# A decoder layer in split precision: first weights loaded and split ahead of constants and squares, the last tile's gate in column groups, spilled activations loaded two blocks earlier

## The chip, the cores and the metric

The kernel runs on one core of one Trainium2 chip. The core has a matrix engine (TensorE, PE in the rows; its weight loads, which overlap matmuls, are listed as PEld), a vector engine (VectorE, DVE), a scalar engine (ScalarE, ACT), GpSimd (POOL) and a sync engine (SyncE, SP), which here issues every plain DMA. Each engine works through its own instructions in program order and waits on semaphores. The metric is device time in microseconds of one execution.

## The reference

One decoder layer for 512 prompt tokens and 64 sample tokens (8 sequences of 8), width 1024, in fp32:

```python
xn = rms_norm(x, attn_norm_g)
z = xn @ w_in                                    # q, k, v, su, sv, gate_a, gate_b
a = window_attention(q, k, v); m = gelu(su) * sgu(layer_norm(gelu(sv)))
h = sigmoid(g_a) * (a @ w_branch_a) + sigmoid(g_b) * (m @ w_branch_b)
x1 = x + h @ w_out
x2 = x1 + peer(rms_norm(x1))                     # see below
gate = sigmoid(rms_norm(x2) @ w_ple_gate)
x3 = x2 + gate * (p_i @ w_ple)
```

`peer` is a product-key retrieval over 16,384 single-neuron experts: 8 heads, the best 16 of each; a token's result is the sum over its experts of gate times gelu(u . x) times the row v.

## The kernel before

**Split matrices.** Every large product is made of three matmuls on fp32r parts: high times high, high times low, low times high. `load_block` (L69) is one weight block of 128 x 1024: a DMA by SP into a ring of four buffers `w_raw`, then `split` (L65): ACT writes `w_hi` (L66, a rounded copy), DVE subtracts to get `w_lo` (L67). These two have a priority offset of 1000 in the scheduler, which sets the order of each engine's instructions when the program is built. Weight blocks pass in the order in which they are written, 3 buffers of `w_hi` and `w_lo` each.

**Start.** x comes transposed as 8 chunks of 128 x 576 (`xT`, names c in the rows; 576 = 512 + 64 tokens). ACT squares them (L140), DVE adds the squares (L142); ACT scales each chunk by the norm's weights and rounds it (L181), DVE makes the low part (L182). PE sums the squares over partitions (L151, each waits for all eight), and a few small steps (L153 to L187) make `rn`, the factor by which each column of a product is multiplied when it leaves PSUM (L192). `w_chunk` (c = 0 to 29) is the projection by one block of 128 columns of `w_in`: 24 matmuls of 256 columns into one PSUM bank, then 24 of 320 into another (`joint`, `tform`, L82), k innermost. `mm` has two banks, so chunk 1 overwrites what chunk 0 had in them. Chunk 0 is k, chunk 1 is v, chunks 2 to 5 are q; after chunk 2 PE transposes v (L249).

**Middle.** Attention, the gating unit, the merge, the expert query and the top-k follow; a long part of it is bound by DVE. Then the prompt's last three tiles of 128 tokens go through all experts densely, 128 blocks of 128 experts: `stage1` makes the activations of a block (`peer_uT`, `xd` in the rows), and `stage2` (the loop over j) multiplies them with the gates `gs` (L974), splits them into `wh` (ACT) and `wl` (DVE) and multiplies by a block of `peer_v` into six PSUM banks `oacc` (L939, 18 matmuls of 512 columns). The other tile and the sample tokens are done by gathers on POOL (`row`, L707) and multiply-adds on DVE (L719), woven in.

**Spilled activations.** The activations of 19 blocks (j = 2, 4, ..., 38) don't fit in SBUF and are in DRAM (`ad`). At the top of the loop over j, the block j + 2 is loaded back (L946, names `x1c<-ad`) into a pool whose x1c tile has 3 buffers. A buffer is read last by the low split `wl<-x1c` of its block. Every 8 blocks SP loads `gs`, 1.5 MB.

**End.** For five tiles (sample, gathered prompt tile, three dense tiles) `tail_gate` (L902) multiplies the normed x2 by `w_pg`, k outermost, both 512-column halves; `tail_out` then does per half a sigmoid (L909), a multiply (L910), an add (L911) and a store (L912).

Of the kernel before, what the change touches and what calls it, by code (L numbers as in the profile page):

```python
# [7 lines left out]
F32 = mybir.dt.float32  # L8
# [3 lines left out]
AF = mybir.ActivationFunctionType  # L12
ALU = mybir.AluOpType
# [15 lines left out]
SPILL = set(range(2, 40, 2))  # L29
# [12 lines left out]
HALVES = (slice(0, 256), slice(256, 576))  # L42
# [5 lines left out]
def tile_decoder_step(ctx: ExitStack, tc: tile.TileContext, a, o):  # L48
    nc = tc.nc
    V, A, T, G, S = nc.vector, nc.scalar, nc.tensor, nc.gpsimd, nc.sync  # L50
# [9 lines left out]
    def cload(name, shape, pl=None):  # L60
        t = (pl or const).tile(shape, F32, name="c_" + name, bufs=1)
        S.dma_start(t, a[name])
        return t
# [2 lines left out]
        A.activation(hi, src, AF.Copy)  # L66
        V.tensor_sub(lo, src, hi.bitcast(F32))  # L67

    def load_block(src, shape=(P, KC, P)):  # L69
        raw = wp.tile(list(shape), F32, name="w_raw", bufs=4)  # L70
        S.dma_start(raw, src)
        hi = wp.tile(list(shape), F32R, name="w_hi", bufs=3)
        lo = wp.tile(list(shape), F32R, name="w_lo", bufs=3)
        with tc.high_priority(offset=1000):
            split(raw, hi, lo)
        return hi, lo

# [14 lines left out]
    def mm():  # L92
        return psM.tile([P, 512], F32, name="mm")
# [7 lines left out]
    pld = dr.tile([NT, D], F32, name="pld")  # L101
    ad = dr.tile([NSP, P, NB], F32, name="ad")
# [16 lines left out]
    def f8(mk, *args):  # L119
        t = [mk(*args), mk(*args)]  # L120
        return [t[k // 4][:, k % 4, :] for k in range(KC)]
# [4 lines left out]
    def bank(tag):  # L126
        return psB.tile([P, 512], F32, name=tag)

    def joint(w, x, out, wk=0, nk=KC, bk=mm):
        for cols in HALVES:  # L130
            ps = bk()[:, :cols.stop - cols.start]
            tform(ps, w, [[xi[k][:, cols] for k in range(nk)] for xi in x], wk, nk)
            out(ps, cols)
# [34 lines left out]

    vecs = cload("vecs", [P, 18])
    xT = f8(f4)  # L170
    for k in range(KC):
        S.dma_start(xT[k], a["xT"][k])
        if k == 1:
            first = load_block(a["w_in"][0])
    ident = cload("ident", [P, P])
    xn = (f8(x4), f8(x4))
    tot, add = sumsq()
    for k in range(KC):
        with tc.high_priority(offset=500):
            add(k, xT[k])  # L180
        A.activation(xn[0][k], xT[k], AF.Copy, scale=vecs[:, k:k + 1])  # L181
        V.scalar_tensor_tensor(xn[1][k], xT[k], vecs[:, k:k + 1], xn[0][k].bitcast(F32),  # L182
                               op0=ALU.mult, op1=ALU.subtract)
    rn = e1.tile([P, NT], F32, name="rn", bufs=1)
    with tc.high_priority(offset=500):
        for cols, ps in rstd_rows(tot, lambda: bank("sc")):
# [2 lines left out]
    def w_chunk(c, dst, out):  # L189
        def scaled(ps, cols):  # L190
            with tc.high_priority(offset=1000):
                V.tensor_tensor(dst[:, cols], ps, rn[:, cols], op=ALU.mult)  # L192
            out(cols)
        joint(load_block(a["w_in"][c]) if c else first, xn, scaled)

    kraw, vTr = tt(), tt()
    w_chunk(0, kraw, lambda cols: None)
# [40 lines left out]
    for g in range(4):  # L238
# [7 lines left out]
        if g == 0:  # L246
            pv = bank("pt")
# [3 lines left out]
            pv = bank("pt")  # L251
# [206 lines left out]
    for i in range(24):  # L458
        if i < 8:
            t, g = (svT, suT)[i // 4], i % 4  # L460
            z = t[:, g, :]
            w_chunk(6 + i, z, lambda cols: A.activation(z[:, cols], z[:, cols], AF.Gelu_apprx_tanh))
        else:
            c, br = divmod(i - 8, 2)
            if (i - 8) % 4 == 0:
                sg4.append(f4())
            sg = sg4[-1][:, (i - 8) % 4, :]
# [15 lines left out]
    hs = ([], [])  # L483
    for c in range(KC):
        w = load_block(a["w_br"][c])
        for i, (x, k0_) in enumerate(((ahl, 0), (mhl, 4))):
            sg = sgs[2 * c + i]
# [20 lines left out]
    for c in range(KC):  # L508
        w = load_block(a["w_out"][c])
# [18 lines left out]
    for c0, r in tilesA:  # L528
# [4 lines left out]
        for hh in range(2):  # L533
            hs = slice(hh * 512, (hh + 1) * 512)
            pt = bank("pt")
            for k in range(4):
                x1k = x1[hh * 4 + k][:, c0:c0 + r]
                T.transpose(out=pt[:r, k * P:(k + 1) * P], in_=x1k, identity=ident)
                if r == NS:
# [3 lines left out]
                                   op0=ALU.mult, op1=ALU.mult)  # L543
# [186 lines left out]
    for i in range(16):  # L730
        h, c = i // 4 + i % 2 * 4, i // 2 % 2
        w = load_block(a["peer_wq"][2 * h + c])
# [134 lines left out]
    d3 = pool(ds, "d3", 3)  # L867
# [27 lines left out]
    def tail_scale(x2, ss, r, xn3):  # L895
        V.scalar_tensor_tensor(xn3[:r], x2[:r], ss[:r], pg[:r], op0=ALU.mult, op1=ALU.mult)

    def tail_gate(w, xh, xl, r, ps):
        for k in range(KC):
            for xi, wi in ((xh, 0), (xh, 1), (xl, 0)):  # L900
                for hh in range(2):
                    T.matmul(ps[hh][:r], lhsT=xi[:, k, :r], rhs=w[k][wi][:, hh * 512:(hh + 1) * 512],  # L902
                             start=k == 0 and xi is xh and wi == 0, stop=k == KC - 1 and xi is xl)

    def tail_out(x2, r, c0, ps, sg, pl):
        S.dma_start(pl[:r], pld[c0:c0 + r])
        for hh in range(2):
            hs = slice(hh * 512, (hh + 1) * 512)
            A.activation(sg[:r, hs], ps[hh][:r], AF.Sigmoid)  # L909
            V.tensor_tensor(sg[:r, hs], sg[:r, hs], pl[:r, hs], op=ALU.mult)  # L910
            V.tensor_tensor(sg[:r, hs], sg[:r, hs], x2[:r, hs], op=ALU.add)  # L911
            S.dma_start(o["y"][c0:c0 + r, hs], sg[:r, hs])  # L912
# [28 lines left out]

    tails, spp, back = [], [], {}
    for j in range(NJ):
        if j + 2 in SPILL:
            back[j + 2] = d3.tile([P, NB], F32, name="x1c")
            S.dma_start(back[j + 2], ad[sorted(SPILL).index(j + 2)])  # L946
        if j and j - 1 not in SPILL and j1 < NJ:
            stage1()
        pay(G2[0] if j1 < NJ else G2[1])
        if j == TAIL0:  # L950
            aLs.close()
            xds.close()
            spp.append(pool(sps, "spare", 2, "right"))
            gather(max(0, P - done[0]), mark_pe[0])
            pg = gp.tile([P, D], F32, name="xr")
            S.dma_start(pg, a["ple_g"])
            tails.append(gathered(0))
        if j == TAIL1:
            gather(1000, mark_pe[0])
        if j == NJ - 2:  # L960
            tails.append(gathered(1))
        if j % JB == 0:
            gsl = gsp[(j // JB + 1) % 2].tile([P, NB // TB, JB, TB], F32, name="gs")
            nb = NB // TB if j else NB // TB - 1
# [12 lines left out]
        split(wf, wh, wl)
        held.append((j, wh, wl, *vw))
        if j != NJ - 2:
            for t in range(3):  # L980
                for hj in held:
                    stage2(t, *hj)
            held.clear()
        if max(SPILL) < j <= max(SPILL) + KC:
            add_x1(j - max(SPILL) - 1)
# [3 lines left out]
    ws = []  # L989
# [21 lines left out]
    banks = [[mm(), mm()]] + [[psC.tile([P, 512], F32, name="oacc") for _ in range(2)] for _ in range(4)]  # L1011

    def finish_tile(i, x2, xh, xl, sg, r, c0):
        tail_gate(ws, xh, xl, r, banks[i])
        tail_out(x2, r, c0, banks[i], sg, tw.tile([P, D], F32, name="pl"))

    finish_tile(0, *tails[1])
    for t, (x2, xn3, ss) in enumerate(xs):
# [110 lines left out]
```

## Time and profile before

| | us |
|---|---|
| median of 3 runs | 1782.16 |
| the three runs | 1780.88, 1782.16, 1788.48 |
| profiled execution | 1776.88 |
| its span in the trace | 1775.1 |

The rows below come from the profiled execution: its span is 1.78 us shorter than its own time, and the median is 5.28 us above that time. Times in rows are us from the start of the span.

### The profile page before, as it was taken

Reading aid. Unit: us, or ns where it says so; the run is one execution under the profiler, and the core shown is the slowest. Engines: PE = TensorE matmul, PEld = TensorE weight load, DVE = VectorE, ACT = ScalarE, POOL = GpSimd, SP = SyncE. Lnnn points to the kernel's source line nnn. Section 1 sums busy time; section 2 is a strip of 40 time slices with the busy share of each in tenths; the row PEclk is TensorE's granted clock in tenths of the full one; section 3 lists DMA queues with packets and bytes.
Section 4 is the critical chain, followed back from the end, with each engine's and each line's share of the span. In section 5 each row is a group of like instructions: output and inputs, shape, how many; then the busy total and the mean of one; then the engine's idle time right before and its main releaser. Section 6 shows DMA issues by size and latency. Waiting matters only on the chain.

```text
span 1775.1 us, 27763 instructions
## 1 busy us (share of the span) xinstructions
PE 1744.3 (98%) x10094; PEld 1575.1 (89%) x10094; DVE 1434.0 (81%) x2876; ACT 867.0 (49%) x1525; POOL 525.9 (30%) x390
## 2 busy tenths in 40 slices
PE   7999999999999899999999999999999999999998
PEld 7988999999999899999988887899899899887876
DVE  6455556548999999999898888998888888999862
ACT  6567444343236698999833333333333333333441
POOL 0000000000002112455245554454544554566300
PEclk9999999999999999999999999999999999999999
DMA  7211233443226577999999999999999999999741
GB/s 242 75 60 38 71 105 122 141 152 106 81 92 225 173 244 235 361 350 355 352 388 367 371 388 364 394 410 369 365 338 360 364 334 331 335 379 376 284 132 70
DMA packets 176457, 457.06 MB, mean 257 GB/s; under 512 B 15552, under 2 KB 76736, under 8 KB 174272
## 3 DMA queue, kind: packets, MB, share of 16 engines
q1 hardware_dynamic: 120736, 253.22, 40.6%
q0 software_dynamic: 55584, 202.07, 30.8%
q8 instruction: 79, 1.29, 0.3%
q14 instruction: 58, 0.48, 0.1%
HBM read 420.18 MB, written 35.78 MB: 257 GB/s over the span
## 4 chain that ended last, share of the span: by engine, by line
PE 77%; issue 7%; DVE 6%; DMA 5%; POOL 3%; ACT 1%; SPq 0%; DVEq 0%; POOLq 0%; ACTq 0%
PE mm L82 36%; PE oacc L939 21%; PE pv L82 5%; POOL row L707 3%; PE sc L822 2%; DMA row<-peer_v,idx 2%; PE pt L822 2%; PE oacc L902 2%; DVE w_lo L67 2%; PE sc L82 1%; DMA x1c<-ad 1%; DVE row L719 1%; DMA row<-peer_u,idx 1%; PE sc L580 1%; PE pv L447 1%
## 5 line engine op out<-in xcount | busy, mean ns | idle before, releaser
L66 ACT ACTIVATE w_hi<-w_raw 128x1024 fp32r<-128x1024 f32 x325 | 343.9, 1059 | 372.9 <-PE mm L82 287.1
L707 POOL DMA_INDIRECT row<-peer_u,idx x192 | 261.1, 1360 | 872.0 <-issue 520.8
L67 DVE TENSOR_TENSOR w_lo<-w_raw,w_hi 128x1024 fp32r<-128x1024 f32 x325 | 396.6, 1221 | 74.0 <-ACT w_hi L66 73.7
L82 PE MATMUL mm<-xd,w_hi 128*128 128x384 f32 x1552 | 405.9, 341 | 0.5 <-ACT w_hi L66 0.5
L82 PE MATMUL mm<-x,w_hi 128*128 128x256 f32 (+1 forms) x1600 | 329.7, 300 | 9.8 <-ACT x L181 9.5
L707 POOL DMA_INDIRECT row<-peer_v,idx x192 | 263.3, 1372 | 231.8 <-DVE acc L726 202.8
L82 PEld LDWEIGHTS mm<-xd,w_hi 128*128 128x128 f32 x1552 | 281.6, 189 | 5.9 <-ACT w_hi L66 0.8
L82 PEld LDWEIGHTS mm<-x,w_hi 128*128 128x128 f32 x1600 | 257.8, 190 | 24.1 <-ACT x L181 10.0
L82 PE MATMUL mm<-xd,w_lo 128*128 128x384 f32 x776 | 264.4, 341 | 3.7 <-DVE w_lo L67 3.7
L726 DVE SCALAR_TENSOR_TENSOR acc<-row,wts,acc 128x1024 f32<-128x1024 f32 x192 | 245.8, 1280 | 5.3 <-DMA row<-peer_v,idx 4.9
L939 PE MATMUL oacc<-w_hi,wl 128*128 128x512 f32 x768 | 242.0, 397 | 3.7 <-DVE wl L67 3.6
L939 PE MATMUL oacc<-w_lo,wh 128*128 128x512 f32 x768 | 242.0, 396 | 0.4 <-DVE w_lo L67 0.4
L939 PE MATMUL oacc<-w_hi,wh 128*128 128x512 f32 x768 | 242.3, 396 | 0.0
L719 DVE SCALAR_TENSOR_TENSOR row<-row,xr 128x1024 f32<-128x1024 f32 x192 | 231.6, 1221 | 11.0 <-DMA row<-peer_u,idx 8.6
L82 PE MATMUL mm<-x,w_lo 128*128 128x256 f32 (+1 forms) x800 | 236.6, 296 | 0.0
L939 PEld LDWEIGHTS oacc<-w_hi,wl 128*128 128x128 f32 x768 | 144.3, 188 | 39.6 <-DVE wl L67 5.5
L939 PEld LDWEIGHTS oacc<-w_lo,wh 128*128 128x128 f32 x768 | 144.4, 188 | 35.5 <-DVE w_lo L67 1.7
L939 PEld LDWEIGHTS oacc<-w_hi,wh 128*128 128x128 f32 x768 | 143.7, 188 | 29.4 <-ACT xr L921 0.8
L82 PEld LDWEIGHTS mm<-x,w_lo 128*128 128x128 f32 x800 | 151.7, 190 | 1.1 <-issue 0.8
L82 PEld LDWEIGHTS mm<-xd,w_lo 128*128 128x128 f32 x776 | 147.0, 189 | 4.7 <-DVE w_lo L67 4.7
L82 PE MATMUL pv<-xd,w_hi 128*128 128x384 f32 x496 | 136.7, 348 | 0.7 <-ACT x L776 0.7
L66 ACT ACTIVATE wh<-x 128x384 fp32r<-128x384 f32 x66 | 34.7, 526 | 162.6 <-PE oacc L939 153.1
(304 smaller groups left out, 2308.8 us busy)
## 6 DMA issues: line engine op xcount, KB each, us to landing
w_raw<-peer_uT SPq DMA_DIRECT2D x128, 512.0 KB
w_raw<-peer_v SPq DMA_DIRECT2D x128, 512.0 KB
gd<-gs SPq DMA_DIRECT2D x24, 1024.0 KB
gs<-gd SPq DMA_DIRECT2D x15, 1536.0 KB
w_raw<-w_in SPq DMA_DIRECT2D x30, 512.0 KB
w_raw<-peer_wq SPq DMA_DIRECT2D x16, 512.0 KB
w_raw<-w_br SPq DMA_DIRECT2D x8, 512.0 KB
w_raw<-w_out SPq DMA_DIRECT2D x8, 512.0 KB
```

Of the source, the lines that this page charges most:

```text
L66: A.activation(hi, src, AF.Copy)
L67: V.tensor_sub(lo, src, hi.bitcast(F32))
L82: mark_pe[0] = T.matmul(ps, lhsT=w[wi][:, wk + k, :], rhs=x[xi][k], start=i == 0, stop=i == n - 1)
L447: T.matmul(ps[:r], lhsT=xi[:, k, :r], rhs=wl_[k][wi][:, hh * 512:(hh + 1) * 512], start=i == 0, stop=i == 5)
L580: T.matmul(ps[:, b * P:(b + 1) * P], lhsT=qp[:, b * P:(b + 1) * P], rhs=sk, start=True, stop=True)
L707: ins = G.indirect_dma_start(out=row_, out_offset=None, in_=table, in_offset=bass.IndirectOffsetOnAxis(ap=ix, axis=0))
L719: V.scalar_tensor_tensor(row_, row_, 1.0, xrs[ti], op0=ALU.mult, op1=ALU.mult, accum_out=dots[:, s:s + 1])
L726: V.scalar_tensor_tensor(accs[ti], row_, wts[:, s:s + 1], accs[ti], op0=ALU.mult, op1=ALU.add)
L822: T.matmul(pt[:, t * P:(t + 1) * P], lhsT=oa[:, t, :], rhs=ob[:, t, :], start=True, stop=True)
L902: T.matmul(ps[hh][:r], lhsT=xi[:, k, :r], rhs=w[k][wi][:, hh * 512:(hh + 1) * 512], start=k == 0 and xi is xh and wi == 0, stop=k == KC - ...
L939: mark_pe[0] = T.matmul(oacc[t][hh], lhsT=wi[:, ts], rhs=vi[:, hh * 512:(hh + 1) * 512], start=j == 0 and last == 0 and vi is vh, stop=j = ...
```

## The change

Three parts. At the start, the block 0 of `w_in` is loaded ahead of x and blocks 1 and 2 ahead of most constants; the scaling and rounding of x gets priority 1500, the squares keep 500; block 0's product runs with k outermost over both halves (new line L205), so that it uses each chunk of x as it comes; chunks 1 and 2 use the PSUM banks `pv` and `pt`, so that they needn't wait until chunk 0 has been scaled. In stage 2, spilled block j + 4 is loaded at the top of the loop instead of j + 2 (at j = 0, blocks 2 and 4). At the end, the last tile's gate is made in three groups of 512, 256 and 256 columns, each with its own 24 matmuls, and the load of `pl` is issued ahead of them.

```diff
-    def load_block(src, shape=(P, KC, P)):
+    def load_block(src, shape=(P, KC, P), urgent=True):
...
-        with tc.high_priority(offset=1000):
+        with tc.high_priority(offset=1000 if urgent else 0):
             split(raw, hi, lo)
...
+    first = [load_block(a["w_in"][0])]
     for k in range(KC):
         S.dma_start(xT[k], a["xT"][k])
-        if k == 1:
-            first = load_block(a["w_in"][0])
+    first.append(load_block(a["w_in"][1]))
     ident = cload("ident", [P, P])
+    first.append(load_block(a["w_in"][2], urgent=False))
...
     for k in range(KC):
-        with tc.high_priority(offset=500):
+        with tc.high_priority(offset=1500):
+            A.activation(xn[0][k], xT[k], AF.Copy, scale=vecs[:, k:k + 1])
+            V.scalar_tensor_tensor(xn[1][k], xT[k], vecs[:, k:k + 1], xn[0][k].bitcast(F32),
+                                   op0=ALU.mult, op1=ALU.subtract)
+    with tc.high_priority(offset=500):
+        for k in range(KC):
             add(k, xT[k])
-        A.activation(xn[0][k], xT[k], AF.Copy, scale=vecs[:, k:k + 1])
-        V.scalar_tensor_tensor(xn[1][k], xT[k], vecs[:, k:k + 1], xn[0][k].bitcast(F32),
-                               op0=ALU.mult, op1=ALU.subtract)
...
-        joint(load_block(a["w_in"][c]) if c else first, xn, scaled)
+        w = first[c] if c < 3 else load_block(a["w_in"][c])
+        if c:
+            joint(w, xn, scaled, bk=(mm, lambda: bank("pv"), lambda: bank("pt"))[c] if c < 3 else mm)
+            return
+        pss = [mm()[:, :cols.stop - cols.start] for cols in HALVES]
+        for k in range(KC):
+            for ps, cols in zip(pss, HALVES):
+                for i, (wi, xi) in enumerate(((0, 0), (0, 1), (1, 0))):
+                    T.matmul(ps, lhsT=w[wi][:, k, :], rhs=xn[xi][k][:, cols], start=k == 0 and i == 0,
+                             stop=k == KC - 1 and i == 2)
+        for ps, cols in zip(pss, HALVES):
+            scaled(ps, cols)
...
-    def tail_out(x2, r, c0, ps, sg, pl):
-        S.dma_start(pl[:r], pld[c0:c0 + r])
-        for hh in range(2):
-            hs = slice(hh * 512, (hh + 1) * 512)
-            A.activation(sg[:r, hs], ps[hh][:r], AF.Sigmoid)
+    def tail_out(x2, r, c0, sg, pl, parts):
+        for p, hs in parts:
+            A.activation(sg[:r, hs], p[:r, :hs.stop - hs.start], AF.Sigmoid)
...
     for j in range(NJ):
-        if j + 2 in SPILL:
-            back[j + 2] = d3.tile([P, NB], F32, name="x1c")
-            S.dma_start(back[j + 2], ad[sorted(SPILL).index(j + 2)])
+        for jb in (2, 4) if j == 0 else (j + 4,):
+            if jb in SPILL:
+                back[jb] = d3.tile([P, NB], F32, name="x1c")
+                S.dma_start(back[jb], ad[sorted(SPILL).index(jb)])
...
-        tail_gate(ws, xh, xl, r, banks[i])
-        tail_out(x2, r, c0, banks[i], sg, tw.tile([P, D], F32, name="pl"))
+        pl = tw.tile([P, D], F32, name="pl")
+        S.dma_start(pl[:r], pld[c0:c0 + r])
+        parts = list(zip(banks[i], (slice(0, 512), slice(512, D))))
+        groups = [parts]
+        if i == 4:
+            groups = [parts[:1], [(banks[i][1], slice(512, 768))], [(banks[0][0], slice(768, D))]]
+        for g in groups:
+            tail_gate(ws, xh, xl, r, g)
+            tail_out(x2, r, c0, sg, pl, g)
```

What ACT does first, before the change (c_92 holds x chunks 0 to 3, c_93 chunks 4 to 7; x_110 and x_111 are their rounded parts; L140 are squares):

```order
L140 ACT_TABLE_LOAD
L140 ACTIVATE rstd<-c_92 128x576
L140 ACTIVATE t<-c_92 128x576
L66 ACTIVATE w_hi<-w_raw 128x1024
L140 ACTIVATE t<-c_92 128x576
L181 ACTIVATE x_110<-c_92,c_vecs 128x576
L140 ACTIVATE t<-c_92 128x576
L140 ACTIVATE t<-c_93 128x576
L181 ACTIVATE x_110<-c_92,c_vecs 128x576
L140 ACTIVATE t<-c_93 128x576 x2
L181 ACTIVATE x_110<-c_92,c_vecs 128x576
```

And with the change (x_122 and x_123 are the rounded parts):

```order
L66 ACT_TABLE_LOAD
L66 ACTIVATE w_hi<-w_raw 128x1024
L181 ACTIVATE x_122<-c_92,c_vecs 128x576 x4
L181 ACTIVATE x_123<-c_93,c_vecs 128x576 x3
L140 ACTIVATE rstd<-c_92 128x576
L181 ACTIVATE x_123<-c_93,c_vecs 128x576
L140 ACTIVATE t<-c_92 128x576
L66 ACTIVATE w_hi<-w_raw 128x1024
L140 ACTIVATE t<-c_92 128x576 x2
L140 ACTIVATE t<-c_93 128x576
L66 ACTIVATE w_hi<-w_raw 128x1024
```

The first block's high part and all rounded x now stand ahead of the squares.

DVE's rows of the same stretch with the change (x_124 and x_125 are the low parts of x):

```order
L67 TENSOR_TENSOR w_lo<-w_raw,w_hi 128x1024
L182 SCALAR_TENSOR_TENSOR x_124<-c_92,c_vecs,x_122 128x576 x4
L182 SCALAR_TENSOR_TENSOR x_125<-c_93,c_vecs,x_123 128x576 x4
L142 TENSOR_TENSOR rstd<-rstd,t 128x576
L67 TENSOR_TENSOR w_lo<-w_raw,w_hi 128x1024
L142 TENSOR_TENSOR rstd<-rstd,t 128x576 x2
L67 TENSOR_TENSOR w_lo<-w_raw,w_hi 128x1024
L142 TENSOR_TENSOR rstd<-rstd,t 128x576 x2
L222 CAST cst<-c_tabs 128x48
L142 TENSOR_TENSOR rstd<-rstd,t 128x576 x2
L67 TENSOR_TENSOR w_lo<-w_raw,w_hi 128x1024
L154 RECIPROCAL rs<-rs 128x5
```

The seven adds now stand behind all eight low parts, with the low parts of blocks 1 and 2 among them; on PE the sums that wait for the last add (L151) stand behind the 48 matmuls of chunk 0 and 41 of chunk 1, where before they stood behind 26 of chunk 0.

SP's rows around the load of spilled block 36, before the change (the first row loads the gates of blocks 32 to 39):

```order
L966 DMA gs<-gd 128x3072
L71 DMA w_raw<-peer_v 128x1024 x2
L946 DMA x1c<-ad 128x384
L71 DMA w_raw<-peer_uT 128x1024
L71 DMA w_raw<-peer_v 128x1024
```

And with the change:

```order
L979 DMA gs<-gd 128x3072
L959 DMA x1c<-ad 128x384
L71 DMA w_raw<-peer_v 128x1024 x2
L71 DMA w_raw<-peer_uT 128x1024
L71 DMA w_raw<-peer_v 128x1024
```

The load of block 36 has passed two blocks of `peer_v`. Seven of the nineteen loads stand one or two blocks of weights earlier in this way (j = 6, 8, 10, 16, 24, 32, 36); the other twelve keep their places.

## Rows read from the trace of the kernel before

**Rows 1.** The page's first part: busy us of each engine, share of the span and instructions.

```profile
PE 1744.3 (98%) x10094; PEld 1575.1 (89%) x10094; DVE 1434.0 (81%) x2876; ACT 867.0 (49%) x1525; POOL 525.9 (30%) x390
```

**Rows 2.** Busy time by stretch: the stretch, its length, then PE, PEld, DVE, ACT and POOL (instructions in brackets), granted TensorE clock, DMA share, GB/s.

```profile
0.00:25.00 25.00, 15.15 (x87) 12.95 (x88) 16.35 (x26) 19.99 (x32) 0.20 (x4) 1.00 0.69 231
600.00:800.00 200.00, 194.31 (x1264) 186.33 (x1263) 197.75 (x473) 182.12 (x412) 66.00 (x45) 0.99 0.87 286
1040.00:1160.00 120.00, 113.33 (x545) 97.14 (x544) 105.16 (x171) 39.46 (x53) 56.80 (x42) 1.00 0.98 382
```

**Rows 3.** The timeline of the start: when, how long, engine, line, operation, in brackets the idle time before it and what ended it.

```profile
1.19 0.90 SPq L172 DMA_DIRECT2D c<-xT  x2
4.19 0.68 ACT L140 ACTIVATE rstd<-c 128x576 f32<-128x576 f32 x1 [2.16 <-DMA c<-xT]
6.23 1.06 ACT L66 ACTIVATE w_hi<-w_raw 128x1024 fp32r<-128x1024 f32 x1 [0.59 <-DMA w_raw<-w_in]
7.77 0.68 ACT L140 ACTIVATE t<-c 128x576 f32<-128x576 f32 x1 [0.49 <-DMA c<-xT]
9.18 0.58 PE L82 MATMUL mm<-x,w_hi 128*128 128x256 f32 x1 [9.18 <-ACT x L181]
```

**Rows 4.** Groups of the first 25 us by line and shape: count, then busy us and mean ns of one, then the idle time before them.

```profile
L182 DVE SCALAR_TENSOR_TENSOR x<-c,c_vecs,x 128x576 fp32r<-128x576 f32 x8 | 6.3, 811 | 0.4 <-ACT x L181 0.3
L181 ACT ACTIVATE x<-c,c_vecs 128x576 fp32r<-128x576 f32 x8 | 5.8, 760 | 0.0
L142 DVE TENSOR_TENSOR rstd<-rstd,t 128x576 f32<-128x576 f32 x7 | 5.3, 756 | 4.7 <-ACT t L140 4.6
L67 DVE TENSOR_TENSOR w_lo<-w_raw,w_hi 128x1024 fp32r<-128x1024 f32 x4 | 4.9, 1222 | 1.9 <-ACT w_hi L66 1.9
L192 DVE TENSOR_TENSOR t<-mm,rn 128x256 f32<-128x256 f32 x1 | 0.4, 418 | 0.0
L187 ACT ACTIVATE rn<-sc 128x256 f32<-128x256 f32 x1 | 0.4, 362 | 0.0
```

**Rows 5.** PE's timeline in the projection, matmuls of 320 and 256 columns.

```profile
12.60 0.47 PE L82 MATMUL mm<-x,w_hi 128*128 128x320 f32 x1
12.86 0.47 PE L82 MATMUL mm<-x,w_lo 128*128 128x320 f32 x1
...
15.12 0.31 PE L82 MATMUL mm<-x,w_lo 128*128 128x320 f32 x1
15.26 0.63 PE L82 MATMUL mm<-x,w_hi 128*128 128x320 f32 x2
...
24.07 0.40 PE L82 MATMUL mm<-x,w_hi 128*128 128x256 f32 x2
24.31 0.28 PE L82 MATMUL mm<-x,w_lo 128*128 128x256 f32 x1
24.43 0.40 PE L82 MATMUL mm<-x,w_hi 128*128 128x256 f32 x2
```

**Rows 6.** PE's timeline: the sums over the squares, and the transposes of v behind chunk 2.

```profile
16.98 1.26 PE L151 MATMUL sc<-ones,rstd 128*64 128x1 f32 x12
...
36.68 0.60 PE L249 MATMUL pt<-c_ident,t 128*128 128x128 f32 x4
```

**Rows 7.** Waits between 850 and 1150 us: who waited for what, total us, times, the longest.

```profile
DVE x1c L974 <- DMA x1c<-ad: 14.7, 9, 4.9
PE oacc L939 <- DVE wl L67: 3.6, 3, 1.3
PE mm L82 <- DVE w_lo L67: 2.5, 1, 2.5
```

**Rows 8.** The timeline around block 36 on SP and DVE.

```profile
1066.49 0.33 SPq L966 DMA_DIRECT2D gs<-gd  x1
1067.62 4.23 SPq L71 DMA_DIRECT2D w_raw<-peer_v  x2
1068.65 0.56 DVE L67 TENSOR_TENSOR wl<-x1c,wh 128x384 fp32r<-128x384 f32 x1
1071.90 0.44 SPq L946 DMA_DIRECT2D x1c<-ad  x1
1075.97 0.56 DVE L67 TENSOR_TENSOR wl<-x,wh 128x384 fp32r<-128x384 f32 x1
1081.44 0.56 DVE L974 TENSOR_TENSOR x1c<-x1c,gs 128x384 f32<-128x384 f32 x1 [4.91 <-DMA x1c<-ad]
```

**Rows 9.** The timeline around block 10: two loads of `peer_v`, the low split of block 4, and the high split of the second load's block.

```profile
899.79 5.35 SPq L71 DMA_DIRECT2D w_raw<-peer_v  x2
903.10 0.55 DVE L67 TENSOR_TENSOR wl<-x1c,wh 128x384 fp32r<-128x384 f32 x1
913.83 1.06 ACT L66 ACTIVATE w_hi<-w_raw 128x1024 fp32r<-128x1024 f32 x1
```

**Rows 10.** The end of the timeline: the last two matmuls, the sigmoids, multiplies and adds of the last tile's halves.

```profile
1768.34 0.63 PE L902 MATMUL oacc<-gh,x 128*128 128x512 f32 x2
1768.81 1.08 ACT L909 ACTIVATE xn<-oacc 128x512 f32<-128x512 f32 x2 [10.11 <-issue]
1769.44 1.29 DVE L910 TENSOR_TENSOR xn<-xn,pl 128x512 f32<-128x512 f32 x2 [8.70 <-ACT xn L909]
1770.65 1.29 DVE L911 TENSOR_TENSOR xn<-xn,x 128x512 f32<-128x512 f32 x2
```

More of the change, by code (lines that the diff above doesn't have):

```diff
@@ L896, in tail_scale, with tail_gate @@
         V.scalar_tensor_tensor(xn3[:r], x2[:r], ss[:r], pg[:r], op0=ALU.mult, op1=ALU.mult)
-    def tail_gate(w, xh, xl, r, ps):
+    def tail_gate(w, xh, xl, r, parts):
         for k in range(KC):
             for xi, wi in ((xh, 0), (xh, 1), (xl, 0)):
-                for hh in range(2):
-                    T.matmul(ps[hh][:r], lhsT=xi[:, k, :r], rhs=w[k][wi][:, hh * 512:(hh + 1) * 512],
+                for p, hs in parts:
+                    T.matmul(p[:r, :hs.stop - hs.start], lhsT=xi[:, k, :r], rhs=w[k][wi][:, hs],
                              start=k == 0 and xi is xh and wi == 0, stop=k == KC - 1 and xi is xl)
-    def tail_out(x2, r, c0, ps, sg, pl):
-        S.dma_start(pl[:r], pld[c0:c0 + r])
-        for hh in range(2):
-            hs = slice(hh * 512, (hh + 1) * 512)
-            A.activation(sg[:r, hs], ps[hh][:r], AF.Sigmoid)
+    def tail_out(x2, r, c0, sg, pl, parts):
+        for p, hs in parts:
+            A.activation(sg[:r, hs], p[:r, :hs.stop - hs.start], AF.Sigmoid)
             V.tensor_tensor(sg[:r, hs], sg[:r, hs], pl[:r, hs], op=ALU.mult)
```

## The prediction, made before the changed kernel had run

> **What bounds the kernel now.** I read the busy shares first. PE works in 98% of the span [rows 1], so a gain can only come from the 31 us in which it doesn't, and from stretches in which it works at half pace. Then I read busy time by stretch, to see where those are. In the first 25 us PE is busy for 15.15; between 1040 and 1160 us it is idle for 6.7 of 120; between 600 and 800 it is DVE that has no slack, with 197.75 of 200 [rows 2]. The change touches the first two and the last 3 us. The middle it leaves alone: there every input comes from the projection, so a start that ends earlier moves PE and DVE alike, and what is won at the start stays won.
>
> **Part 1, the start: −3.3 us (between −1.0 and −4.5).** In the timeline PE's first matmul is at 9.18, though x and the weights are there from 4.19 on: ACT squares before it scales [rows 3]. What is won is the distance to a place that both kernels must reach; I take the transposes of v behind chunk 2, now at 36.68 [rows 6].
>
> First arrivals. A chunk of x (0.295 MB) issued at 1.19 is used at 4.19, 3.0 us later. x1 and w0, 0.82 MB in all, take the next 2.04 us, to 6.23: 400 GB/s [rows 3]. With w0 (0.524 MB) in x0's place it lands 0.23 MB later than x0 did, at about 4.8; the eight chunks of x follow at 0.74 each, x0 at 5.5 and x7 at 10.7, or 0.7 later if they lag as x2 did (7.77 in place of 6.97) [rows 3]. ACT: w0's high part 1.06 [rows 3] to 5.85, x0's high part 0.76 [rows 4] to 6.6. PE begins at about 6.65 instead of 9.18.
>
> Then DVE: w0's low part 1.22, from 5.95 to 7.15, and eight low parts of x at 0.811 [rows 4], to 13.65. Behind them stand seven adds at 0.756 and two low parts of weights at 1.222, 7.7 us, and a cast: the last square is added at about 21.6. PE by then: in the trace matmuls of 320 columns start 0.26 us apart at 12.60 (320 columns in that time is the 1.2 GHz level, though the column of the granted clock has 1.00 for the stretch [rows 2]) and 0.14 apart at 15.12 (2.4 GHz) [rows 5], so PE is slow for the first 5.9 us of its work. With the same 5.9 us, of eight steps of k (three matmuls of 256 and three of 320, 1.41 slow and 0.76 fast; the first waits 0.45 for x0's low part) four are slow and four fast: chunk 0 ends at 15.9. Matmuls of 256 columns start 0.118 apart [rows 5], so 41 matmuls of chunk 1 (24 x 0.118 + 17 x 0.147, 320 columns by the same pace) end at 21.2. There PE meets the sums, which wait for DVE until 21.6. So DVE and not PE sets this place; a slow stretch that is 0.8 us longer would cost PE 0.4 and the sum nothing.
>
> Before, from the sums at 16.98 to the transposes at 36.68 took 19.7 us [rows 6], with 118 projection matmuls between them. Now 55 are left; the 63 that have gone ahead (35 of 256, 28 of 320) are 8.2 us. So 21.6 + 19.7 − 8.2 = 33.1; I add 0.3, since the reciprocal behind the sums now stands behind one more low part of weights (1.22, of which the trip to ACT and back covers most). 33.4 against 36.68 is −3.3. Upper bound: PE is never kept waiting and its pace is fast a little sooner, −4.5. Lower bound: x lags 0.7 and two more splits (1.05 to 1.22 each) slip ahead of the last add or of `rn`, −1.0.
>
> A page speaks against part of this. The Trainium skill ("TensorE: Matmul & The Clock Gate", Part 1) says that the number of matmuls at the slow clock varies from run to run. The trace has the slow pace (0.26) but only one run of it. Were the slow stretch 3 us longer, PE would reach the sums 1.5 later, at 22.7, and the sum below would lose 1.1; that lies in the bounds.
>
> The constants now come behind w_in's blocks. They are wanted first by the small steps behind the sums (one table for a cast excepted), and `ident` stands right behind block 1: nothing for them.
>
> **Part 2, the spilled blocks: −3.5 us (between 0 and −6.1).** The list of waits between 850 and 1150 has DVE waiting nine times for `x1c`, 14.7 us, once 4.91; PE waits 2.5 for a low part of weights, and 3.6 in three pieces for `wl` [rows 7]. The timeline gives the place: block 36's load is issued at 1071.90, behind the gates at 1066.49 (1.5 MB) and two blocks of weights, and DVE gets it at 1081.44, 9.5 us later; it would have gone on at 1076.5 [rows 8].
>
> "Two blocks ahead" is not what the load gets. The pool has three x1c buffers in both kernels, so the load of block 36 waits for `wl` of block 30, which ends at 1069.21 [rows 8]. The order shows the effect that is left: it now stands right behind the gates, ahead of two blocks of weights. It is issued at 1069.2, 2.7 earlier, with 1.05 MB less before it (2.6 us at 400 GB/s). The two overlap in part, so it lands 3.1 to 4.7 earlier, at 1076.7 to 1078.3. DVE then waits 0.2 to 1.8 in place of 4.91. PE's wait of 2.5 at that place goes wholly, and DVE keeps some 2 us that PE did not need; of PE's three later waits, 3.6 us, I let this take 1.0. 2.5 + 1.0 = 3.5. The upper bound takes all 3.6; the lower one is nothing, if the two blocks of weights that were passed come just as late as block 36 did. The other six moved loads end waits of DVE that PE doesn't feel: beside these four, the list has no wait of PE for DVE that `x1c` could set [rows 7]. The other twelve keep their place: nothing.
>
> **Part 3, the end: −1.8 us (between −1.5 and −3.0).** The last two matmuls end at 1768.97. Two sigmoids (1.08 for both), two multiplies (1.29) and two adds (1.29) of 512 columns follow, the last of them until 1771.94: 2.97 us behind PE [rows 10]. PE's own time is unchanged: 512 columns take 0.235 (0.47 for two [rows 10]) and 256 take 0.118 [rows 5], so 48 of the one are 24 of the one and 48 of the other. Now only 256 columns follow: from PSUM a 256-column copy took 0.362 on ACT and a multiply 0.418 on DVE [rows 4]. One of each and an add of at most 0.42 are 1.2, if the sigmoid starts right at PE's end. So the gain is 2.97 − 1.2 = 1.8, or 1.5 with two handovers of 0.15. The last store has half the bytes; between the last add at 1771.94 and the span's end lie 3.2 us, and I count nothing for them, with −1.2 as the bound. The Trainium skill ("DMA: Bandwidth & Descriptors", Anatomy of one DMA) gives a fixed part of about 2.0 us and a part by size; by it the 128 KB less would be 0.3.
>
> **Sum.** −3.3 − 3.5 − 1.8 = −8.6. The profiled execution took 1776.88 (1.78 more than its span), so a like one takes 1768.3; the median of the runs shown lies 5.28 above the profiled execution, so 1782.16 − 8.6 = 1773.6.
>
> **Rivals.**
> (a) More: PE's later waits for `wl` vanish too (−6.1), the start gives its bound of −4.5, the end −2.2: −12.8, 1769.4. For it: DVE is late in that stretch by less than the 4.91 that it lost. Against: those waits come with new gathers and another load of gates in between.
> (b) The change of the spilled blocks does nothing, because the three buffers hold the load back anyway and what it passes comes as late: −5.1, 1777.1. For it: 382 GB/s and a DMA share of 0.98 in that stretch [rows 2]; what is moved forward moves something back.
> (c) The start is eaten: everything that needs `rn` waits for the squares, which now come last on ACT and DVE, and PE idles behind the sums: −1.0 − 3.5 − 1.8 = −6.3, 1775.9.
> (d) Slower. SP works in order, and the load that now stands ahead of blocks of `peer_v` waits for a `wl`. At block 10, `peer_v` was issued at 899.79; `wl` of block 4 ends only at 903.65 [rows 9], so it would now go at 904.0, 4.2 later; at block 36 the first goes at 1069.6 instead of 1067.62, 1.9 later [rows 8]. Five such places at 3.05 on average are 15; if all reach PE, 15.2 − 3.3 − 1.8 = +10, 1792.3. It decides where a block lands later than its split: for block 10's second load 913.83 − 904.0 = 9.8 us after issue [rows 9], and the longest trip that I see is 9.5 [rows 8]; so it doesn't, barely. The Trainium skill ("DMA: Bandwidth & Descriptors", Anatomy of one DMA) has the rule behind it: a wait on a semaphore is taken by the sequencer that issues, ahead of dispatch. Were it to bite here, the time is the one just given.
>
> **Chances.** My forecast 0.55 (own range 1771.5 to 1775.7), (a) 0.17, (b) 0.13, (c) 0.10, (d) 0.05. The range 1768 to 1780 takes in (a), (b) and (c) with a little for the scatter of the three runs, and leaves out (d) and mixtures beyond (a). 0.5%, about what a measurement of this kernel can tell from no change, is 8.9 us, and my sum is 8.6: the line runs through the middle of the forecast. Faster by more: (a) and half of the forecast, 0.45; within: the other half, (b) and (c) and a little of (d), 0.48; slower 0.07.
>
> **What would show it.** Start: PE's first matmul at 6.6, L205's last near 15.9, sums at 21.6, transposes at 33.4. Stage 2: DVE's wait for block 36 below 2 us, no PE wait of 2.5 near it, no new wait of ACT for `peer_v`. End: last add 1.2 to 1.5 behind PE's last matmul. I am wrong if PE idles over 1 us behind the sums, if the waits for `wl` grow, or if the stretch from 50 to 850 us takes longer than before.

## The result, and the profile after

| | before | after |
|---|---|---|
| median of 6 runs, us | 1780.42 | 1765.41 |
| lowest and highest | 1777.46 to 1788.48 | 1764.70 to 1767.91 |
| profiled execution | 1776.88 | 1767.91 |
| its span | 1775.1 | 1766.1 |

The ratio is 0.9915 (0.9897 to 0.9933): 15.1 us faster (11.9 to 18.3). I had said 1773.6 with a range from 1768.0, so the time lies 2.6 us below the range. Of the 8.2 us between forecast and measurement 1.7 come from the start of the sum: before's median is 1782.16 over three runs and 1780.42 over six. The other 6.5 are the gain, 15.1 in place of 8.6. Yet from one profiled execution to the other the gain is 9.0 us, and there my sum was −8.6 (1768.3 forecast, 1767.91 measured). Both are measurements. The trace of before came from an execution 3.5 us below the median of its kernel, that of after from one 2.5 us above: that difference of 6 us is what the experiments had to explain.

Busy shares after, to be held against [rows 1]:

```profile
PE 1741.2 (99%) x10118; PEld 1574.5 (89%) x10118; DVE 1436.6 (81%) x2878; ACT 868.3 (49%) x1526; POOL 518.3 (29%) x390
```

PE is idle for 24.9 us in place of 30.8. Busy time by stretch after (columns as in [rows 2]):

```profile
0.00:25.00 25.00, 17.97 (x115) 17.41 (x116) 16.45 (x24) 18.16 (x25) 0.20 (x4) 1.00 0.83 299
600.00:800.00 200.00, 196.33 (x1278) 188.12 (x1278) 196.89 (x473) 183.06 (x416) 66.50 (x45) 0.99 0.88 291
1040.00:1160.00 120.00, 117.74 (x578) 102.98 (x577) 111.44 (x179) 41.56 (x56) 57.55 (x44) 1.00 1.01 403
```

In the first stretch PE did 115 matmuls instead of 87, in the third 578 instead of 545. The start after, in the timeline of PE and with DVE's last two adds (answers to [rows 3, 5, 6]; L205 is chunk 0, `pv` chunk 1, L142 the adds, L151 the sums, L263 the transposes):

```profile
6.56 0.85 PE L205 MATMUL mm<-x,w_hi 128*128 128x256 f32 x2 [6.56 <-ACT x L181]
7.88 0.58 PE L205 MATMUL mm<-x,w_hi 128*128 128x256 f32 x1 [0.47 <-DVE x L182]
...
16.62 0.40 PE L82 MATMUL pv<-x,w_hi 128*128 128x256 f32 x2
...
20.01 1.62 DVE L142 TENSOR_TENSOR rstd<-rstd,t 128x576 f32<-128x576 f32 x2
...
22.04 1.26 PE L151 MATMUL sc<-ones,rstd 128*64 128x1 f32 x12
...
33.38 0.61 PE L263 MATMUL pt<-c_ident,t 128*128 128x128 f32 x4
```

Forecast were 6.65 for the first matmul, 15.9 for the end of chunk 0 (measured 16.6), 21.6 for the last add (21.63) and the sums (22.04, without a wait of PE), and 33.4 for the transposes (33.38, against 36.68). Block 36 after (answers to [rows 8]):

```profile
1062.18 0.33 SPq L979 DMA_DIRECT2D gs<-gd  x1
1064.35 0.55 DVE L67 TENSOR_TENSOR wl<-x1c,wh 128x384 fp32r<-128x384 f32 x1
1064.93 0.33 SPq L959 DMA_DIRECT2D x1c<-ad  x1
1065.31 2.23 SPq L71 DMA_DIRECT2D w_raw<-peer_v  x2
1072.50 0.56 DVE L987 TENSOR_TENSOR x1c<-x1c,gs 128x384 f32<-128x384 f32 x1 [0.28 <-DVE wl L67]
```

The load goes 0.03 us after `wl` of block 30 ends (1064.90), as the three buffers would have it, with the two `peer_v` behind it, and DVE no longer waits for it. Waits between 850 and 1150 us after (answers to [rows 7]):

```profile
DVE x1c L987 <- DMA x1c<-ad: 9.0, 5, 4.5
...
PE oacc L951 <- DVE wl L67: 2.3, 2, 1.6
...
PE oacc L951 <- ACT wh L66: 1.3, 1, 1.3
```

PE's wait of 2.5 for the low part of weights is gone and the 3.6 for `wl` have become 2.3; the 1.3 stands at the start of stage 2, where the first trace of before has no wait (a second one has 2.9, see below). ACT's waits for `peer_v` between 850 and 1150 us are 3.1 us in three pieces (2.4 in three before). The end after (answers to [rows 10]):

```profile
1761.69 0.28 PE L916 MATMUL mm<-gh,x 128*128 128x256 f32 x1
1762.01 0.38 ACT L921 ACTIVATE xn<-mm 128x256 f32<-128x256 f32 x1 [2.38 <-PE mm L916]
1762.42 0.42 DVE L922 TENSOR_TENSOR xn<-xn,pl 128x256 f32<-128x256 f32 x1 [1.87 <-ACT xn L921]
1762.88 0.43 DVE L923 TENSOR_TENSOR xn<-xn,x 128x256 f32<-128x256 f32 x1
```

The last add ends at 1763.31, 1.34 us behind PE (2.97 before), and the span ends 2.79 later (3.16 before): −2.0.

### The profile page after: what moved, and what is told of

Its sections match the earlier page's. It is cut to its first block, busy times and chain, and to the rows that moved or that the text cites. A ratio compares the mean times of both kernels' runs of the same rounds, so it can differ in the third digit from the quotient of the medians.

```text
span 1766.1 us, 27818 instructions
## 1 busy us (share of the span) xinstructions
PE 1741.2 (99%) x10118; PEld 1574.5 (89%) x10118; DVE 1436.6 (81%) x2878; ACT 868.3 (49%) x1526; POOL 518.3 (29%) x390
## 2 busy tenths in 40 slices
DMA packets 176601, 457.07 MB, mean 259 GB/s; under 512 B 15568, under 2 KB 77008, under 8 KB 174416
## 3 DMA queue, kind: packets, MB, share of 16 engines
q0 software_dynamic: 55584, 202.07, 30.8%
## 4 chain that ended last, share of the span: by engine, by line
PE 81%; issue 6%; DVE 5%; DMA 4%; POOL 3%; ACT 1%; SPq 0%; POOLq 0%; DVEq 0%; ACTq 0%
PE mm L82 36%; PE oacc L951 24%; PE pv L82 5%; POOL row L721 3%; PE oacc L916 2%; PE sc L836 2%; PE pt L836 2%; DMA row<-peer_u,idx 2%; DMA row<-peer_v,idx 2%; PE sc L82 1%; DVE w_lo L67 1%; PE sc L594 1%; PE pv L461 1%; PE mm L916 1%; PE pv L329 1%
## 5 line engine op out<-in xcount | busy, mean ns | idle before, releaser
L721 POOL DMA_INDIRECT row<-peer_v,idx x192 | 256.6, 1337 | 240.5 <-DVE acc L740 215.2
L82 PE MATMUL mm<-x,w_hi 128*128 128x320 f32 (+1 forms) x1504 | 305.4, 297 | 0.0
L82 PEld LDWEIGHTS mm<-x,w_hi 128*128 128x128 f32 x1504 | 239.3, 188 | 12.5 <-issue 9.0
L82 PE MATMUL mm<-x,w_lo 128*128 128x320 f32 (+1 forms) x752 | 220.6, 294 | 0.0
L82 PEld LDWEIGHTS mm<-x,w_lo 128*128 128x128 f32 x752 | 141.1, 188 | 1.1 <-issue 0.8
```

The lines of the kernel that those rows point to most:

```text
L82: mark_pe[0] = T.matmul(ps, lhsT=w[wi][:, wk + k, :], rhs=x[xi][k], start=i == 0, stop=i == n - 1)
L721: ins = G.indirect_dma_start(out=row_, out_offset=None, in_=table, in_offset=bass.IndirectOffsetOnAxis(ap=ix, axis=0))
```

## Experiments

Each time is the median against the kernel before on the same chip, worked out from the ratio; the interval is that of the ratio times before's median.

**before_again: the kernel before, unchanged.**

> The kernel before once more, unchanged: it shows how far executions of one kernel lie apart. Theory A (the two traces tell the whole of it, 9.0 us of span, and the six runs of before merely scattered upwards): the median of this one is again near 1777 to 1780 and its trace agrees with the first within 1 us at every place. Theory B (before has a stall of changing size, of which the first trace shows a small case): the new trace is 3 to 6 us longer than the first, and the difference sits in one or two places, most likely DVE's wait for spilled blocks between 1040 and 1160 us or a stretch of half TensorE clock between 60 and 100 us.

1778.98 (1774.67 to 1785.31 in 12 runs), ratio 1.0 (0.9989 to 1.0011). Its trace is 7.2 us longer than the first, and the difference sits in two places: theory B, though this execution lies 5.1 us above the median of its twelve and so shows a large case. Its waits between 850 and 1150 us, and PE's timeline behind the longest of them:

```profile
DVE x1c L974 <- DMA x1c<-ad: 13.2, 6, 5.8
...
PE mm L82 <- DVE w_lo L67: 4.3, 1, 4.3
```

```profile
1091.22 0.69 PE L82 MATMUL mm<-xd,w_lo 128*128 128x384 f32 x1 [4.32 <-DVE w_lo L67]
1091.71 0.84 PE L82 MATMUL mm<-xd,w_hi 128*128 128x384 f32 x2
1092.35 0.52 PE L82 MATMUL mm<-xd,w_lo 128*128 128x384 f32 x1
1092.67 0.84 PE L82 MATMUL mm<-xd,w_hi 128*128 128x384 f32 x2
...
1096.84 0.34 PE L82 MATMUL mm<-xd,w_lo 128*128 128x384 f32 x1
1097.01 0.50 PE L82 MATMUL mm<-xd,w_hi 128*128 128x384 f32 x2
1097.35 0.34 PE L82 MATMUL mm<-xd,w_lo 128*128 128x384 f32 x1
```

The same wait as in [rows 7, 8], but PE is idle for 4.32 us instead of 2.5. And what follows is slow: three matmuls of 384 columns take 0.96 us from 1091.71 to 1092.67, so 0.32 each (384 columns at 1.2 GHz), until some 5 us later they are 0.17 apart again (1096.84 to 1097.01, 2.4 GHz). Those 5 us cost 2.5 beside the wait. In the first trace of before the same matmuls, behind a shorter wait, were fast. A second such place, behind a wait of 2.9 us for the first gates, lies at 885 us, and it is the larger one: between 850 and 900 us PE is idle for 2.9 us (0.01 in the first trace) and the granted clock is 0.93, which is 3.5 us lost. Between 1040 and 1160 us PE is idle as long as in the first trace (6.64 and 6.67), since the later waits are shorter, and only the clock differs.

**e1_start, e2_spill, e3_end: each part alone** (the three parts of the diff above).

> The start alone. My sum: -3.3 us, the transposes of v at 33.4. Theory A adds nothing. Theory C: the half clock that the trace of before shows at 76.5 to 79.9 us and the changed kernel's doesn't is gone because of the start's change, and -1.3 to -1.7 come on top, -5 in all. Rival: it is chance, and this kernel's trace shows it in some place too.

> The earlier loads of spilled blocks alone. My sum: -3.5 us with bounds 0 and -6.1. The traces show -6.2 between 1080 and 1125 us, after a loss of 2.3 between 790 and 885 us: theory A, -4 to -6. Theory B: -8 to -10, because the wait for block 36 in before is often longer than the 4.9 us of the first trace.

> The last tile's column groups alone. My sum: -1.8 us with bounds -1.5 and -3.0; the last add then ends 1.2 to 1.5 us behind PE's last matmul and the span's end lies 3.2 behind it as before. Rival: the final store is quicker by up to 1.2 with half the bytes: -3.

| | median, us | ratio | against before, us |
|---|---|---|---|
| start | 1775.63 | 0.9981 (0.9968 to 0.9994) | −3.4 (−5.7 to −1.1) |
| spilled blocks | 1770.74 | 0.9950 (0.9937 to 0.9964) | −8.9 (−11.2 to −6.4) |
| end | 1776.94 | 0.9983 (0.9972 to 0.9994) | −3.0 (−5.0 to −1.1) |

They add up to −15.3, as the whole measured. The start is as large as I had it. Theory C falls: e1's trace has the half clock near 73 us too (granted clock 0.97 between 50 and 100 us, as in the first trace of before), and in that of before_again it is missing: it comes and goes with no change. The end's −3.0 has my −1.8 and the trace's −2.0 in its interval. The spilled blocks are far from −3.5 and outside its bounds.

**s36: the load of block 36 alone.**

```diff
-        if j + 2 in SPILL:
-            back[j + 2] = d3.tile([P, NB], F32, name="x1c")
-            S.dma_start(back[j + 2], ad[sorted(SPILL).index(j + 2)])
+        for jb in (j + 2, 36) if j == 32 else (j + 2,):
+            if jb in SPILL and jb not in back and j != 34:
+                back[jb] = d3.tile([P, NB], F32, name="x1c")
+                S.dma_start(back[jb], ad[sorted(SPILL).index(jb)])
```

> The kernel before with one change: the load of spilled block 36 is issued at the top of j = 32, right behind the load of gates, as in the changed kernel; the other 18 loads stay where they were. Theory: that one load is all of the spill part, which measured -8.9 us alone: -7 to -10 here, DVE's wait for block 36 below 1 us and no half clock between 1080 and 1130 us. Rival: the six other moved loads carry a share: -3 to -6.

1772.78, ratio 0.9968 (0.9958 to 0.9979): −5.7 (−7.5 to −3.7), in the rival's range, with an interval that reaches into the theory's. DVE's multiply of block 36 waits for nothing, and there is no half clock between 1040 and 1160 us.

**n_spill (start and end without the spilled blocks) and after_again (the changed kernel once more).**

> The changed kernel with the loads of spilled blocks as before (start and end only). By the single parts, -3.4 and -3.0: -6.4 us, and the wait for block 36 of 4 to 6 us is back. Rival: the parts help each other (a start that ends earlier moves the half clock's windows elsewhere): -9 or more.

> The changed kernel once more: -14 to -15 us against before, and again no half clock between 800 and 1200 us; if that was chance in the first trace, there is one here.

n_spill: 1770.97, ratio 0.9956 (0.9943 to 0.9969), −7.8 (−10.1 to −5.5); DVE's wait for block 36 is 5.2 us again. after_again: 1765.66, ratio 0.9929 (0.9913 to 0.9944), −12.6 (−15.5 to −10.0), and no half clock. In company the spilled blocks are worth −4.8 by these two. after_again came out 1.4 short of what I expected, with it inside the interval.

**fill78: matmuls of no use inside PE's wait.**

```diff
         ps = (mm() if j % 2 or phase[0] > 1 else bank("pv"))[:, :NB]
+        for _ in range(14 if j == 78 else 0):
+            T.matmul(ps, lhsT=w[0][:, 0, :], rhs=xb[0][0], start=True, stop=True)
         tform(ps, w, xb)
```

> The kernel before with 14 more matmuls of 384 columns, written into a PSUM bank that the next matmul starts anew, in PE's queue just ahead of the matmul that waits 2.5 to 4.3 us at about 1084 us: 14 x 0.17 = 2.4 us of work inside a wait that ends no sooner. The output is the same. Theory (PE's idle time there is followed by a stretch at half clock in most executions, which is what the first trace didn't show): no half clock within 10 us behind that wait, and -1 to -3 us. Rival (the half clock there is chance, or the wait is all of the loss): 0 to +0.5.

1778.78, ratio 1.0003 (0.9991 to 1.0015): +0.5 (−1.6 to +2.7). The trace shows what was meant:

```profile
1085.93 2.59 PE L769 MATMUL mm<-xd,w_hi 128*128 128x384 f32 x14
1088.36 0.51 PE L82 MATMUL mm<-xd,w_hi 128*128 128x384 f32 x2
1089.16 0.45 PE L82 MATMUL mm<-xd,w_lo 128*128 128x384 f32 x1 [0.29 <-DVE w_lo L67]
1089.44 0.51 PE L82 MATMUL mm<-xd,w_hi 128*128 128x384 f32 x2
1089.79 0.34 PE L82 MATMUL mm<-xd,w_lo 128*128 128x384 f32 x1
```

PE goes on at full pace behind it. But the time didn't fall: the +0.5 is the rival's figure. In an execution with a short wait (in e3's trace there was none over 0.3 us at this place) the 2.6 us are pure cost, which may eat what they win in others; that isn't shown. So this run doesn't price the half clock, and the rival (the wait is all of the loss) isn't excluded by it.

**e2_again, a_s36, after_third: does it have to be all seven loads?** a_s36 is the changed kernel with s36's edit in place of its own loop.

> The earlier loads of spilled blocks alone, once more, on the same chip as the next two. Alone they measured -8.9 us, the one load of block 36 -5.7, and the changed kernel minus the one without them -4.8. Theory (one size, about -6, with chance in the first figure): -5 to -7. Rival (the six other loads matter as well): -8 to -10 again.

> The changed kernel, but of the loads of spilled blocks only that of block 36 is moved; the other 18 are as before the change. Theory (block 36 is all of it): within 1 us of the changed kernel, -12 to -14 against before. Rival (the six others are worth 2 to 3): -10.

> The changed kernel beside the two others, so that they are compared on one chip: -12 to -15 us.

| | median, us | ratio | against before, us |
|---|---|---|---|
| e2_again | 1771.20 | 0.9954 (0.9938 to 0.9970) | −8.2 (−11.0 to −5.3) |
| a_s36 | 1767.07 | 0.9932 (0.9914 to 0.9949) | −12.1 (−15.3 to −9.1) |
| after_third | 1765.60 | 0.9922 (0.9905 to 0.9940) | −13.9 (−16.9 to −10.7) |

e2_again came in its rival's range, and a_s36 1.8 behind the changed kernel where my theory had 1; both intervals hold the theory too. All seven loads beat block 36 alone by 2.5 to 3.2 us on the plain kernel and by 1.8 in the changed one; each difference lies within the intervals. That block 36 makes most of it is shown; whether the six others are worth 2 us stays open.

**a_gs: the first load of gates in two pieces.**

```diff
-                S.dma_start(gsl[:, :nb], gd[j // JB][:, :nb])
+                for js in (slice(0, 2), slice(2, JB)) if j == 0 else (slice(0, JB),):
+                    S.dma_start(gsl[:, :nb, js], gd[j // JB][:, :nb, js])
```

> The changed kernel with the first load of gates in two pieces, those of blocks 0 and 1 first. In most traces PE waits 0.8 to 3.0 us at the start of stage 2, because DVE's first multiply waits for that load of 1.5 MB, and in two of them a stretch of half clock follows. If the first piece is there in time, the wait goes and nothing takes its place: -1 to -2 us against the changed kernel. Rival: pieces of 128 bytes are slow, and the second piece comes later than the whole did: 0 to +2.

1771.92, ratio 0.9949 (0.9931 to 0.9967): −9.1 against before, so 4.8 behind after_third by the ratios. In its timeline:

```profile
871.64 2.13 SPq L980 DMA_DIRECT2D gs<-gd  x2
...
876.81 1.03 DVE L988 TENSOR_TENSOR x<-x,gs 128x384 f32<-128x384 f32 x2 [5.42 <-DMA gs<-gd]
...
961.66 0.56 DVE L988 TENSOR_TENSOR x1c<-x1c,gs 128x384 f32<-128x384 f32 x1 [4.23 <-DMA x1c<-ad]
...
964.61 0.73 PE L951 MATMUL oacc<-w_lo,wh 128*128 128x512 f32 x2 [2.44 <-DVE w_lo L67]
```

DVE still waits for the first piece, 5.42 us, and a spilled block comes late at 961.66, with a wait of PE behind it (964.61); between 900 and 1040 us no other kernel's trace has a wait of PE over 1 us. In that stretch PE is idle for 3.4 us and the granted clock is 0.99, where after_third has no idle time and 1.00. My theory falls, and the loss is larger than the rival's 0 to 2; that the pieces cause the late spilled block isn't shown.

## Why the prediction was wrong

**The half clock and the wait's size, over all traces.** The stretch from 1040 to 1160 us in each kernel's own trace (columns as in [rows 2]), five with block 36's load late (before is in [rows 2], four follow), then seven with it early (after stands above, six follow); fill78 and a_gs, which change something else, are left out.

before_again, load late:

```profile
1040.00:1160.00 120.00, 113.36 (x536) 98.67 (x535) 104.37 (x167) 39.09 (x52) 54.90 (x41) 0.97 0.98 380
```

e1_start, load late:

```profile
1040.00:1160.00 120.00, 114.03 (x535) 98.54 (x534) 103.67 (x165) 38.71 (x53) 55.80 (x41) 0.97 0.97 378
```

e3_end, load late:

```profile
1040.00:1160.00 120.00, 117.30 (x560) 100.97 (x559) 106.21 (x170) 40.56 (x54) 56.80 (x42) 0.99 0.99 389
```

n_spill, load late:

```profile
1040.00:1160.00 120.00, 115.17 (x548) 100.22 (x548) 104.81 (x170) 38.78 (x53) 54.56 (x41) 0.97 0.98 382
```

e2_spill, load early:

```profile
1040.00:1160.00 120.00, 117.24 (x573) 102.39 (x572) 109.88 (x176) 40.91 (x55) 57.78 (x44) 1.00 1.01 401
```

e2_again, load early:

```profile
1040.00:1160.00 120.00, 117.84 (x575) 102.69 (x574) 111.01 (x179) 41.29 (x55) 58.19 (x43) 1.00 1.01 401
```

s36, load early:

```profile
1040.00:1160.00 120.00, 117.11 (x572) 101.98 (x571) 109.78 (x179) 41.28 (x55) 56.35 (x43) 1.00 1.01 400
```

a_s36, load early:

```profile
1040.00:1160.00 120.00, 116.52 (x571) 101.33 (x570) 108.96 (x174) 40.81 (x55) 56.20 (x42) 1.00 1.00 395
```

after_again, load early:

```profile
1040.00:1160.00 120.00, 117.19 (x576) 102.43 (x575) 110.55 (x178) 40.67 (x54) 57.03 (x42) 1.00 1.01 396
```

after_third, load early:

```profile
1040.00:1160.00 120.00, 119.03 (x588) 104.55 (x587) 112.51 (x181) 42.07 (x56) 59.81 (x44) 1.00 1.02 409
```

Late, PE is idle for 2.7 to 6.7 us (mean 5.4) and the granted clock is below 1.00 in four of five, 0.98 on average: 2.4 us of 120 lost at the 1.2 GHz level. Early, it is idle for 1.0 to 3.5 (mean 2.5) and the clock is 1.00 in all seven. So the part is worth 2.9 of idle time and 2.4 of clock there, 5.3 in all. The one trace that I had was the exception with the clock at 1.00.

Not all of this lies at block 36. The 35 us around it, five times with the load late (before, before_again, e1_start, e3_end, n_spill), then once with it early (after):

```profile
1065.00:1100.00 35.00, 32.11 (x152) 27.15 (x152) 30.09 (x49) 11.12 (x15) 15.75 (x11) 1.00 0.93 353
1065.00:1100.00 35.00, 30.68 (x135) 26.68 (x134) 28.45 (x45) 10.54 (x14) 15.68 (x12) 0.90 0.88 322
1065.00:1100.00 35.00, 31.61 (x142) 27.25 (x142) 29.11 (x48) 10.97 (x15) 14.83 (x12) 0.95 0.90 339
1065.00:1100.00 35.00, 34.52 (x164) 29.34 (x163) 30.67 (x50) 12.04 (x16) 16.39 (x12) 1.00 0.93 356
1065.00:1100.00 35.00, 31.99 (x149) 28.25 (x148) 29.56 (x49) 11.18 (x15) 17.72 (x13) 0.95 0.93 355
1065.00:1100.00 35.00, 35.00 (x171) 30.62 (x170) 32.80 (x52) 12.32 (x17) 19.48 (x15) 1.00 1.02 405
```

Here PE is idle for 0.5 to 4.3 us when the load is late (mean 2.8) and for 0 to 0.4 when it is early (mean 0.1), and the late ones lose 1.4 us of clock on average. Behind 1100 us the idle time is the same, 2.5 and 2.4; the other 1.0 of clock is lost near 1120 us in e1_start, e3_end and n_spill, and that it follows from block 36 isn't shown. All runs together give a smaller price for the clock than these traces. Its mean over the whole span rises from before's 0.9960 to 0.9972 in e2_spill, from 0.9953 to 0.9963 in e2_again, from 0.9964 to 0.9971 in s36, and from n_spill's 0.9973 to 0.9977 in after_again. That is 2.0, 1.8, 1.4 and 0.6 us.

Over the whole of stage 2, from its first product to PE's last matmul, the five late traces take 883.3 to 890.6 us (mean 886.7), the seven early ones 878.4 to 881.4 (mean 880.4): 6.3 us, of which 1.0 lies outside 1040 to 1160 us.

The Trainium skill ("TensorE: Matmul & The Clock Gate", Part 1) says that PE's rest state is the throttled one and that activity releases it; the slow pace behind the 4.32 us of before_again agrees, while the 2.5 us in [rows 7] passed without it, so no gap length follows from these traces.

By point:
- **Part 1, right in size, partly by luck.** −3.3 forecast, −3.30 at the transposes, −3.4 timed (−5.7 to −1.1). DVE's last add ended at 21.63, as forecast, but in this trace PE and not DVE set the place: its slow stretch lasted until 13.3, 6.8 us and not 5.9, chunk 0 ended 0.7 late, and PE met the sums at 22.04 without a wait. In four of the seven traces with the new start it does wait for DVE there, 0.3 to 0.6. The steps behind the sums took 11.3 us where I had 11.8, which made up for it. And 36.68 is the earliest that the old start shows: its seven traces have the transposes at 36.7 to 38.4 (mean 37.4), the seven with the new one at 32.7 to 33.4 (mean 33.0), −4.4. From there to stage 2 both take about as long (847.0 and 847.2 on average), so what was won stayed won, though the trace of after alone took 1.2 longer than that of before. (Two slips in the working: 7.77 in place of 6.97 is a lag of 0.8, not 0.7, and chunk 0's steps add up to 15.8, not 15.9.) Rival (c) falls: PE doesn't idle over 1 us behind the sums, and 600 to 800 us keeps its 2% to 3% of PE idle.
- **Part 2, the mechanism right, its size wrong: here the prediction failed.** The place in SP's order, the wait for `wl` of block 30, DVE's wait of 0.2 to 1.8 (0.28) and the end of PE's wait of 2.5 came as written. The step that failed is "PE's wait of 2.5 at that place goes wholly, and ... I let this take 1.0. 2.5 + 1.0 = 3.5": it prices PE's idle time in one execution and has no term for matmuls that go at half clock. The 2.5 was 2.8 on average, the 1.0 for the later waits 0.1, and the clock, 2.4 by the traces and 0.6 to 2.0 by the runs, isn't in the sum. Over all of stage 2 the traces give 6.3; alone the part timed −8.9 and −8.2, in company −4.8. What lies between 6.3 and 8.9 isn't settled (the six other loads, or chance).
- **Part 3, right.** −1.8 forecast; −2.0 in the traces, of which 0.37 is the shorter way from the last add to the span's end. I had counted nothing for that; the estimate by the Trainium skill ("DMA: Bandwidth & Descriptors", Anatomy of one DMA), 0.3, is closer, though its fit is for DMAs that GpSimd issues and this store is issued by SP. Timed −3.0, with −2.0 inside.
- **The sum, wrong in its last line.** "The median of the runs shown lies 5.28 above the profiled execution, so 1782.16 − 8.6" treats these 5.28 us as a constant that both kernels have. They weren't: after's median lies 2.5 below its profiled execution. What they are made of is shown only in part. The trace of before had its transposes 0.7 earlier than the mean of the old start, a stage 2 that was 1.0 shorter than the mean of the late ones, and, unlike before_again, no wait at 885 us.
- **Rivals.** (b) falls by the trace. (d) too: the first `peer_v` does stand behind the wait, as the rule of the Trainium skill that I had named for it ("DMA: Bandwidth & Descriptors", Anatomy of one DMA) says, issued at 1065.31 behind 1064.93, and PE's list has no wait for a block of `peer_v`. (a) is nearest in size, 1769.4, and over all traces its three figures, 6.1, 4.5 and 2.2, come near the 6.3, 4.4 and 2.0 found, but not by its mechanism: PE's waits for `wl` shrank from 3.6 to 2.3 in the first pair of traces and did not vanish, and on average PE's idle time there hardly changed. The chances gave faster by over 0.5% 0.45; their sum has a slip, as half of the forecast with (b) and (c) is already 0.505 and not 0.48.

## What to carry to other kernels

A wait's size in one profiled execution is a sample. Where the medians lie several us above the profiled execution, ask which waits grow in the slower runs before taking the difference for a constant, and take a second trace of the unchanged kernel: it showed 4.3 us where the first had 2.5. A gap on PE is priced with the matmuls behind it, by their distance in the rows, and the granted clock of the stretch tells whether they were slow. In a queue that issues in order, one small load that stands behind two large ones can cost more than all the others together (here 5.7 us for one, some 2 to 3, not settled, for the six others); its place is worth more than how many blocks ahead it is asked for. A part that comes out to a tenth of a us, as my start did, may have been met by one lucky trace: take several there too.

## What I had not expected of the hardware

The same program had a granted clock of 1.00 in one trace and 0.97 in the next, between 1040 and 1160 us, at the same instructions (before and before_again; whether on the same chip isn't on record). Its twelve runs spread over 10.6 us (1774.67 to 1785.31), those of the changed kernel, six each, over 3.2 to 7.6 (1764.70 to 1767.91, 1762.49 to 1770.08). And a load of a quarter of the size was not four times as quick. The first piece of the gates in a_gs, 368 KB, was used 5.2 us after its issue (871.64 to 876.81), with DVE waiting for it; the whole load of 1,472 KB in the changed kernel, with DVE waiting for it too, 7.0 us after (873.12 to 880.09):

```profile
873.12 0.33 SPq L979 DMA_DIRECT2D gs<-gd  x1
...
880.09 1.50 DVE L987 TENSOR_TENSOR x<-x,gs 128x384 f32<-128x384 f32 x3 [1.22 <-DMA gs<-gd]
```

This isn't the size alone: the first piece goes in runs of 128 bytes (a_gs moved 21,472 packets under 512 bytes, after_third 15,568), and the second piece, three times as large, is issued right behind it. Which of these counts no run here separates.
